# Which operand stands in the array: the experts' second product of a two-layer encoder kernel

## The chip, the cores and the metric

One Trainium2 chip, one core of it. The metric is the device time of one execution in microseconds; the profile comes from one execution that the hardware profiler recorded. Engines are named as in the profile: PE (TensorE, its weight loads apart as PEld), DVE (VectorE), ACT (ScalarE), POOL (GpSimd), SP (SyncE, which issues most of the DMAs).

## What is computed

Two encoder layers on 256 tokens of 1024 channels. Each layer is a token-mixing sub-layer and then a product-key expert sub-layer, both wrapped in a residual and a LayerNorm. The change lies in the second product of the expert sub-layer. The reference picks 16 of 16384 experts per head and token and then computes

```python
act = jax.nn.gelu(jnp.einsum('cd,chkd->chk', hc, u_tab[ic]))
w = (gc * act.astype(jnp.float32)).astype(hc.dtype)
return jnp.einsum('chk,chkd->cd', w, v_tab[ic])
...
x <- LayerNorm(ALPHA * x + gate * sublayer(x * (1 + scale) + shift))
```

The kernel does not gather: it computes all 16384 activations against the table U, multiplies them by a dense matrix of weights that is zero for experts that were not picked, and multiplies the result W (16384 experts x 256 tokens) by the table V (16384 x 1024).

## The kernel before

The program is a list of jobs (loop at L1203 to L1234). A job of a large product has a block of 128 x 1024 float32 weights in DRAM (512 KB), which SP loads into a tile `raw` (three buffers, L1171). ACT rounds it to a high part `whi` (`split_hi`, L238) and DVE computes the low part `wlo` as the difference (`split_lo`, L241); both have three buffers (LOOK + 1) and are made two jobs ahead, so ACT writes the `whi` of job k + 2 into the buffer that job k - 1 has left. Each product is taken in three passes, low x high, high x low and high x high, in float32r, all added up in PSUM. Everything between the large products (top-k, expert weights, attention) is issued in steps beside them; a scheduler of the framework puts the instructions of each engine in order, by priorities of its own, and the orders shown below are its result.

The expert sub-layer of each layer l has 16 query jobs, 128 jobs of U (`u_job`, L1038) and then 128 jobs of V (`v_job`, L1069). The 256 columns of W for each job stand in the big tiles GA, GB0, GB1 and GB2 as [expert, token]. `pre` splits one such [128, 256] block into a pair `wv` (ACT and DVE, tiles with the tags e0, e1 and pts). Then `three(m, ...)` takes channel chunk m = 0..7: the 128 x 128 block of V is the stationary operand, the 256 tokens move, and the sum stands in PSUM as [channel, token], two chunks to a bank, in banks 0 to 3 (`acc4`):

```python
o = state["acc4"][m // 2][:, m % 2]
PE.matmul(o, hi[:, m], wl, ...)
PE.matmul(o, lo[:, m], wh, ...)
PE.matmul(o, hi[:, m], wh, ...)
```

That is 24 matmuls per job, each with a weight load of its own, in L1080 to L1082. The last three jobs (VLAST) are held back and taken chunk by chunk, nine matmuls for each chunk, so that the end of the sub-layer can begin on chunk 0 while chunk 7 is multiplied. `ln2` (L1125) adds each chunk, scaled, to the residual r (L1130), and `stats` sums r and r squared over the chunks (ACT L305 and L309, DVE L311 and L315, tile `lnss`); `norm` then forms the sums over partitions on PE (L339), a Newton chain on DVE (L320 to L324), broadcasts (L327) and two passes over r (L358). In layer 1 the next layer's first products follow, in layer 2 the output.

Hooks on the V jobs carry other work: at jobs 1 and 3 `make_cact` loads the conditioning vector (`crow`, by a DMA on ACT's queue) and multiplies it out on PE (`cb`, L166), and 8 to 24 times a layer DVE forms a column of the modulation from 512 KB of `w_ada` (L260). At job 110 `load_r` claims the tile `raws`, in the space of GA, and `r`.

Of the kernel before, what the change touches and what calls it, by code (L numbers as in the profile page):

```python
# [11 lines left out]
F32 = mybir.dt.float32  # L12
# [10 lines left out]
NC8 = 8  # L23
# [3 lines left out]
NAREA = 3           # products whose weights are split ahead of a norm  # L27
NCAND = 4 * 16 + 12 * 4     # pairs (i, j) of ranks with i < 4 or j < 4: any other has more than 16 ahead of it
LATE = 320 + DEPTH * 384
VLAST = 3           # of the experts' last products, taken chunk by chunk  # L30
GSCALE = 4096.0      # on the experts' weights while they are float16 pairs

# columns of the packed parameters
# [3 lines left out]
# columns of the packed constants  # L37
# [3 lines left out]
# chunks of 128 columns of w_in  # L41
# [3 lines left out]
# order in which the chunks of the modulation are made: (scale, shift) of the first sub-layer, then the rest  # L45
# [3 lines left out]
class Background:  # L49
    """Chains of small operations, taken step by step between the large products."""  # L50
# [4 lines left out]
    def add(self, make):  # L55
        """make(lane) gives the generator of the steps"""
        self.pending.append(make)
# [12 lines left out]
    def round(self):  # L70
        """a step of each lane; false when there was none"""
        return any([self.step(i) is not None for i in range(len(self.active))])

    def run(self, budget):
        """steps for about this much time; what they took more"""
        while budget > 0:
            c = self.step(0)
            if c is None:
                return 0.0
            budget -= c  # L80
        return -budget


class InOrder:
    """an engine whose instructions keep their place among those emitted before"""
# [30 lines left out]
def _body(tc, nc, A, pp, big, hp, st, wk, ps, dr, stop, dump):  # L116
# [6 lines left out]
    # ---------------------------------------------------------------- set-up  # L123
    prm = pp.tile([128, NPRM], F32, name="prm")
    nc.sync.dma_start(prm, A["prm"])
    xd = dr.tile([128, NC8, T], F32, name="xd")      # ALPHA x, away from the chip while a sub-layer runs
# [16 lines left out]
    fold = pp.tile([128, 2, 2, NC8], F32, name="fold")   # scale and shift of the next layer's input; of the residual  # L143
# [4 lines left out]
    def make_cact(parts=(0, 1)):  # L148
        """silu(c) on all partitions"""
# [21 lines left out]
    def late_setup():  # L171
# [13 lines left out]
        # lambda of the differential attention  # L185
# [12 lines left out]
        # softplus(-lam) = max(-lam, 0) + log1p(exp(-|lam|)), log1p by the series of atanh  # L198
# [7 lines left out]
        V.tensor_tensor(w[:, 2], w[:, 1], w[:, 3], op=OP.mult)          # z  # L206
        V.tensor_tensor(w[:, 3], w[:, 2], w[:, 2], op=OP.mult)          # z^2
# [9 lines left out]
    # ---------------------------------------------------------------- helpers  # L217
# [12 lines left out]
    def drain_small():  # L230
        """what the products before the last one left"""
# [11 lines left out]
    def prod(out, whi, wlo, xhi, xlo, n, start=True, stop=True):  # L243
        """out[m, t] += sum over n chunks of w[k, c, m] x[k, c, t], in three passes"""
# [19 lines left out]
    def mains(ks):  # L264
        """banks of the large products, in turn"""
        state["banks"] = cycle(ks)
# [7 lines left out]
    def new_areas(tag, more=0):  # L274
        """room for the weights of the first products after a norm"""
# [12 lines left out]
    def behind(*ins):  # L288
        """what follows waits its turn behind these"""
# [10 lines left out]
    def stats(r, m, direct):  # L300
        """sums of r and r^2 over the chunks so far; the last chunks of r are left to norm's products"""
# [15 lines left out]
    def rsqrt(y, hv):  # L317
        """y = (2 hv)^-1/2 of two columns: Newton's steps from the exponent's estimate; each turns the sign"""
# [10 lines left out]
    def norm(r, emit):  # L329
        """(r - mean) / std in place, emit(m) after each chunk"""  # L330
# [31 lines left out]
    def norm_to_h(r, hi, lo, sc, sh, g, b):  # L362
        """h = (norm * g + b) * (1 + sc) + sh, split; xd = ALPHA (norm * g + b)"""
# [20 lines left out]
    # ---------------------------------------------------------------- jobs  # L384
# [3 lines left out]
    def areas_of(js, before, n):  # L388
        """the areas of js filled after the job n of those before, and split after each next one"""
# [36 lines left out]
    def layer(l):  # L426
        pv = lambda o, w=1: prm[:, o:o + w]

        # ------------------------------------------------ token mixing
# [65 lines left out]
        def bchunk(a, k):  # L495
            """chunk k of the branches' outputs, its high or low part"""
# [7 lines left out]
        def to_keys(e, lane):  # L504
            """p^T [key, chunk of keys, query]"""
# [24 lines left out]
        def pair(lane, branch, c):  # L530
            """two heads of the branches A and B"""
# [210 lines left out]
        # ------------------------------------------------ gated merge  # L742
# [35 lines left out]
        # the rest of the modulation, but for the gate of the experts  # L778
# [44 lines left out]
        # ------------------------------------------------ product-key experts  # L823
        def peer_begin():
# [23 lines left out]
            # over the scores, once they are ranked  # L848
# [14 lines left out]
        def top16(sets):  # L863
            """the 16 largest and their places, for independent sets in turn"""
# [27 lines left out]
        def select_gen():  # L892
# [17 lines left out]
            # the place p in cand: i = p / 16, j = p mod 16 below 64; then i = p / 4 - 12, j = p mod 4  # L910
# [19 lines left out]
            for t in range(2):  # L930
                tt = slice(t * 128, (t + 1) * 128)
                for i in range(2):
# [6 lines left out]
                    # one term of each sum is not zero  # L939
# [19 lines left out]
        def slots(lo, hi):  # L959
            """pieces of the expert columns lo..hi"""  # L960
# [7 lines left out]
        def weights_gen():  # L968
# [5 lines left out]
            def onehots(t0):  # L974
                """rows of the weights in two parts (exact to float32's last place), and columns"""
# [88 lines left out]
        def v_begin():  # L1064
            drain()
            state["acc4"] = [bank(k, [128, 2, T], name="vacc") for k in range(4)]
        jobs.append(Job(func=v_begin))

        def v_job(j):  # L1069
# [8 lines left out]
            def three(m, hi, lo, wh, wl, first, last):  # L1078
                o = state["acc4"][m // 2][:, m % 2]
# [245 lines left out]
```

## Time and profile before

| | |
|---|---|
| three runs | 2422.90, 2424.97 and 2426.39 us, median 2424.97 us |
| profiled execution | 2424.2 us from the first to the last instruction (the profile gives no other time of it) |
| PE matmul busy | 98% of the span, 19540 matmuls |
| PE weight loads busy | 95%, 19540 loads |
| DVE, ACT busy | 77% and 53% |
| V jobs, matmuls | 3 x 2048; those of L1080 start from 837.5 to 1212.4 us and from 2032.9 to 2404.4 us |

The matmul's duration in the profile (0.28 us) runs from its start to the end of its last column's way through the array, and several are under way at once; what a matmul costs in a stream is the distance from one start to the next. "PEclk" and the third column from the right of a table by stretches give the clock that was granted to TensorE: 1.00 is 2.4 GHz, 0.50 is 1.2 GHz. "<-" in brackets names who ended an engine's idle time.

### The profile page before, as it was taken

Reading aid. Unit: us, or ns where it says so; the run is one execution under the profiler, and the core shown is the slowest. Engines: PE = TensorE matmul, PEld = TensorE weight load, DVE = VectorE, ACT = ScalarE, POOL = GpSimd, SP = SyncE. Lnnn points to the kernel's source line nnn. Section 1 sums busy time; section 2 is a strip of 40 time slices with the busy share of each in tenths; the row PEclk is TensorE's granted clock in tenths of the full one; section 3 lists DMA queues with packets and bytes.
Section 4 is the critical chain, followed back from the end, with each engine's and each line's share of the span. In section 5 each row is a group of like instructions: output and inputs, shape, how many; then the busy total and the mean of one; then the engine's idle time right before and its main releaser. Section 6 shows DMA issues by size and latency. Waiting matters only on the chain.

```text
span 2424.2 us, 49848 instructions
## 1 busy us (share of the span) xinstructions
PE 2367.3 (98%) x19540; PEld 2298.4 (95%) x19540; DVE 1871.2 (77%) x4056; ACT 1281.7 (53%) x2535; POOL 0.2 (0%) x4
## 2 busy tenths in 40 slices
PE   6999999999999999999989999999999999999997
PEld 5988999999999999999988889899999999999997
DVE  8687788989999656666677877889899996655555
ACT  5755545456554444445467564455555554444443
POOL 0000000000000000000000000000000000000000
PEclk9999999999999999999989999999999999999998
DMA  8465763454444566767533756545554455655553
GB/s 328 151 210 202 252 227 130 165 190 158 157 160 157 191 205 218 243 219 261 192 132 129 263 183 244 200 149 183 167 165 158 160 165 194 219 201 184 184 200 106
DMA packets 127638, 460.64 MB, mean 190 GB/s; under 512 B 15398, under 2 KB 20006, under 8 KB 124204
## 3 DMA queue, kind: packets, MB, share of 16 engines
q1 hardware_dynamic: 126816, 453.25, 55.0%
q8 instruction: 155, 2.54, 0.4%
q10 hardware_dynamic: 588, 4.21, 0.4%
q14 instruction: 79, 0.65, 0.1%
HBM read 448.75 MB, written 5.24 MB: 187 GB/s over the span
## 4 chain that ended last, share of the span: by engine, by line
PE 85%; DVE 12%; issue 1%; ACT 1%; DMA 1%; SPq 0%; ACTq 0%; DVEq 0%
PE main L246 16%; PE main L247 16%; PE main L248 16%; PE vacc L1080 10%; PE vacc L1081 10%; PE vacc L1082 10%; DVE wlo L241 3%; PE s L520 2%; DVE topk L92 1%; DVE GA L1005 1%; PE gw L995 1%; PE o L576 1%; DVE ada L260 1%; PE gw L996 1%; DVE GB L1005 1%
## 5 line engine op out<-in xcount | busy, mean ns | idle before, releaser
L241 DVE TENSOR_TENSOR wlo<-raw,whi 128x1024 fp32r<-128x1024 f32 x723 | 879.1, 1217 | 394.0 <-ACT whi L238 390.5
L246 PE MATMUL main<-hhi,wlo 128*128 128x256 f32 x3456 | 999.5, 289 | 0.6 <-DVE wlo L241 0.6
L238 ACT ACTIVATE whi<-raw 128x1024 fp32r<-128x1024 f32 x720 | 760.7, 1057 | 436.4 <-PE vacc L1082 370.6
L247 PE MATMUL main<-hlo,whi 128*128 128x256 f32 x3456 | 978.1, 283 | 0.0
L248 PE MATMUL main<-hhi,whi 128*128 128x256 f32 x3456 | 978.1, 283 | 0.0
L246 PEld LDWEIGHTS main<-hhi,wlo 128*128 128x128 f32 x3456 | 662.4, 192 | 5.4 <-DVE wlo L241 2.2
L247 PEld LDWEIGHTS main<-hlo,whi 128*128 128x128 f32 x3456 | 662.5, 192 | 1.3 <-issue 0.8
L248 PEld LDWEIGHTS main<-hhi,whi 128*128 128x128 f32 x3456 | 661.9, 192 | 0.7 <-issue 0.7
L1080 PE MATMUL vacc<-wv,whi 128*128 128x256 f32 x2048 | 580.7, 284 | 0.0
L1081 PE MATMUL vacc<-wv,wlo 128*128 128x256 f32 x2048 | 580.6, 284 | 0.0
L1082 PE MATMUL vacc<-wv,whi 128*128 128x256 f32 x2048 | 580.5, 284 | 0.0
L1080 PEld LDWEIGHTS vacc<-wv,whi 128*128 128x128 f32 x2048 | 394.1, 193 | 2.6 <-DVE wlo L241 1.5
L1081 PEld LDWEIGHTS vacc<-wv,wlo 128*128 128x128 f32 x2048 | 394.2, 192 | 0.0
L1082 PEld LDWEIGHTS vacc<-wv,whi 128*128 128x128 f32 x2048 | 394.2, 192 | 0.0
L1052 ACT ACTIVATE gel<-main 128x256 f32<-128x256 f32 (+20 forms) x192 | 56.6, 295 | 228.2 <-PE main L248 227.7
L1009 ACT ACTIVATE GB<-gw 128x128 f32<-128x128 f32 (+15 forms) x316 | 71.9, 339 | 49.8 <-DVE GB L1005 49.4
L1005 DVE TENSOR_TENSOR GA<-gw,GA 128x256 f32<-128x256 f32 (+17 forms) x128 | 88.4, 691 | 1.2
L995 PE MATMUL gw<-ohb,oha 128*128 128x128 f16 x512 | 72.0, 222 | 1.0 <-ACT GB L1009 0.4
L247 PE MATMUL main<-mixB,whi 128*128 128x256 f32 x256 | 72.5, 283 | 0.0
L248 PE MATMUL main<-mixB,whi 128*128 128x256 f32 x256 | 72.5, 283 | 0.0
L246 PE MATMUL main<-mixB,wlo 128*128 128x256 f32 x256 | 72.5, 283 | 0.0
L724 ACT ACTIVATE mixG<-main,hbg 128x256 f32<-128x256 f32 x64 | 30.2, 472 | 76.7 <-PE main L248 76.5
(228 smaller groups left out, 2409.6 us busy)
## 6 DMA issues: line engine op xcount, KB each, us to landing
raw<-in_p_u SPq DMA_DIRECT2D x256, 512.0 KB, 3.4
raw<-in_p_v SPq DMA_DIRECT2D x256, 512.0 KB, 3.6
raw<-in_w_in SPq DMA_DIRECT2D x134, 512.0 KB, 3.9
mixA<-in_w_ada SPq DMA_DIRECT2D x48, 512.0 KB, 4.6
raw<-in_w_br SPq DMA_DIRECT2D x32, 512.0 KB, 3.8
adav<-in_w_ada SPq DMA_DIRECT2D x32, 512.0 KB, 4.4
raw<-in_p_wq SPq DMA_DIRECT2D x26, 512.0 KB, 3.5
ada<-in_w_ada SPq DMA_DIRECT2D x8, 1024.0 KB, 11.9
```

Source lines behind the costliest of these rows:

```text
L238: return S.activation(hi, src, AF.Copy, scale=scale)
L241: return V.tensor_tensor(lo, src, hi.bitcast(F32), op=OP.subtract)
L246: PE.matmul(out, wlo(c), xhi(c), start=start and c == 0, stop=False)
L247: PE.matmul(out, whi(c), xlo(c), start=False, stop=False)
L248: PE.matmul(out, whi(c), xhi(c), start=False, stop=stop and c == n - 1)
L995: PE.matmul(p[:, k], a[:, 0, k], b[:, k], start=True, stop=False)
L1005: V.tensor_tensor(o, p[:, :, x:x + n], o, op=OP.mult)
L1009: S.activation(sl[:, :, t0:t0 + NB].rearrange("p j t -> p t j"), p[:, :, x:x + n], AF.Copy)
L1052: S.activation(t[:, :n], out[:, :n], AF.Gelu_apprx_tanh)
L1080: PE.matmul(o, hi[:, m], wl, start=first and m % 2 == 0, stop=False, skip_group_check=True)
L1081: PE.matmul(o, lo[:, m], wh, start=False, stop=False, skip_group_check=True)
L1082: PE.matmul(o, hi[:, m], wh, start=False, stop=last, skip_group_check=True)
```

## The change

In the V jobs the two operands change places. The stationary operand is now a 128 x 128 block of `wv` (experts x tokens, one of two halves of the tokens), and rows of V move, 512 of their 1024 columns at a time. The sum stands in PSUM as [token, channel], one bank for each pair of token half (b % 2) and channel half (b // 2). A job takes four groups of three matmuls with 512 columns in place of eight groups of three with 256.

Because LayerNorm and all that follows want [channel, token], the four sums are copied to SBUF (`take`, ACT for b = 0 and 2, DVE for b = 1 and 3, 128 x 512 each, into 2048 more columns of `raws`) and turned by 16 transposes of 128 x 128 on PE (`turn`), into banks 4, 5, 6 and 0. `ln2` reads those. The three held jobs are taken bank by bank, and the transposes of bank b - 1 follow the matmuls of bank b.

```diff
-            state["acc4"] = [bank(k, [128, 2, T], name="vacc") for k in range(4)]
+            state["acc4"] = [bank(k, [128, 512], name="vacc") for k in range(4)]
...
-            def three(m, hi, lo, wh, wl, first, last):
-                o = state["acc4"][m // 2][:, m % 2]
-                PE.matmul(o, hi[:, m], wl, start=first and m % 2 == 0, stop=False, skip_group_check=True)
-                PE.matmul(o, lo[:, m], wh, start=False, stop=False, skip_group_check=True)
-                PE.matmul(o, hi[:, m], wh, start=False, stop=last, skip_group_check=True)
+            def three(b, hi, lo, wh, wl, first, last):
+
+                o = state["acc4"][b]
+                tt = slice(b % 2 * 128, b % 2 * 128 + 128)
+                hi, lo = (x.rearrange("p c m -> p (c m)")[:, b // 2 * 512:b // 2 * 512 + 512] for x in (hi, lo))
+                PE.matmul(o, wl[:, tt], hi, start=first, stop=False)
+                PE.matmul(o, wh[:, tt], lo, start=False, stop=False)
+                PE.matmul(o, wh[:, tt], hi, start=False, stop=last)
...
                 elif j == 127:
-                    for m in range(NC8):
+                    for b in range(4):
                         for i, x in enumerate(held):
-                            three(m, *x, False, i == VLAST - 1)
+                            three(b, *x, False, i == VLAST - 1)
+                        take(b)
+                        if b:
+                            turn(b - 1)
+                    turn(3)
...
+        def take(b):
+            out = state["raws"][:, NAREA * D + 512 * b:NAREA * D + 512 * (b + 1)]
+            if b % 2:
+                V.tensor_copy(out, state["acc4"][b])
+            else:
+                S.activation(out, state["acc4"][b], AF.Copy)
+
+        def turn(b):
+
+            if b % 2 == 0:
+                ks = (4, 5) if b == 0 else (6, 0)
+                state["turned", b // 2] = [bank(k, [128, 2, T], name="vt") for k in ks]
+            for q in range(4):
+                o = NAREA * D + 512 * b + 128 * q
+                PE.transpose(state["turned", b // 2][q // 2][:, q % 2, b % 2 * 128:b % 2 * 128 + 128],
+                             state["raws"][:, o:o + 128], ident)
+
         def load_r():
             r = new_chunks("r2")
-            new_areas("gA")
+            new_areas("gA", 2048)
...
-                V.scalar_tensor_tensor(r[:, m], state["acc4"][m // 2][:, m % 2], gq[:, m:m + 1], r[:, m],
+                V.scalar_tensor_tensor(r[:, m], state["turned", m // 4][m % 4 // 2][:, m % 2], gq[:, m:m + 1], r[:, m],
```

Where the instructions move, PE's order first: the start of a V job in the middle of layer 1, before (vacc0 and vacc1 are banks 0 and 1 of the sums).

```order
L1080 MATMUL vacc0_10939<-wv_12271,whi_12241 128x256 [waits DVE_49,Activation_49]
L1081 MATMUL vacc0_10939<-wv_12271,wlo_12242 128x256 [waits DVE_49]
L1082 MATMUL vacc0_10939<-wv_12271,whi_12241 128x256
L1080 MATMUL vacc0_10939<-wv_12271,whi_12241 128x256
L1081 MATMUL vacc0_10939<-wv_12271,wlo_12242 128x256
L1082 MATMUL vacc0_10939<-wv_12271,whi_12241 128x256
```

And the same place with the change.

```order
L1083 MATMUL vacc0_10939<-whi_11785,wv_11803 128x512 [waits DVE_49,Activation_49]
L1084 MATMUL vacc0_10939<-wlo_11786,wv_11803 128x512 [waits DVE_49]
L1085 MATMUL vacc0_10939<-whi_11785,wv_11803 128x512
L1083 MATMUL vacc1_10940<-whi_11785,wv_11803 128x512
L1084 MATMUL vacc1_10940<-wlo_11786,wv_11803 128x512
L1085 MATMUL vacc1_10940<-whi_11785,wv_11803 128x512
```

Three matmuls of 512 columns now fill a bank where six of 256 did, and the waits for ACT and DVE stand at the same two instructions of a job. The second place is PE at the end of layer 2 with the change, from the last matmuls on bank 3 (vt4, vt5, vt6 and vt0 are the turned sums in banks 4, 5, 6 and 0; cst holds the identity).

```order
L1085 MATMUL vacc3_24565<-whi_27217,wv_27233 128x512
L1083 MATMUL vacc3_24565<-whi_27236,wv_27240 128x512
L1084 MATMUL vacc3_24565<-wlo_27237,wv_27240 128x512
L1085 MATMUL vacc3_24565<-whi_27236,wv_27240 128x512
L1118 MATMUL vt6_27293<-cst_82,raws_26938 128x128 [waits Activation_49]
L1118 MATMUL vt6_27293<-cst_82,raws_26938 128x128
L1118 MATMUL vt0_27294<-cst_82,raws_26938 128x128 x2
L1118 MATMUL vt6_27293<-cst_82,raws_26938 128x128 [waits DVE_49]
L1118 MATMUL vt6_27293<-cst_82,raws_26938 128x128
L1118 MATMUL vt0_27294<-cst_82,raws_26938 128x128 x2
L339 MATMUL lnst7_27341<-ones_87,lnss_27306 128x1 [waits DVE_49]
L339 MATMUL lnst7_27341<-ones_87,lnss_27306 128x1
```

Before, the last matmul on vacc3 is followed at once by L339; now eight transposes stand between, four that wait for ACT's copy of bank 2 and four that wait for DVE's copy of bank 3. The eight of banks 0 and 1 stand ahead of bank 3's nine matmuls, behind those of bank 1 and of bank 2. The third place is DVE at the end of layer 2, before, from the last split to where its work on r and the sums over chunks repeats.

```order
L241 TENSOR_TENSOR wlo_30249<-raw_30157,whi_30248 128x1024 [waits DMAHW7_49,Activation_49]
L1130 SCALAR_TENSOR_TENSOR r2_29780<-vacc0_26074,gq_30327,r2_29780 128x256 [waits PE_49]
L1130 SCALAR_TENSOR_TENSOR r2_29780<-vacc0_26074,gq_30327,r2_29780 128x256
L1130 SCALAR_TENSOR_TENSOR r2_29780<-vacc1_26075,gq_30327,r2_29780 128x256 [waits PE_49]
L1130 SCALAR_TENSOR_TENSOR r2_29780<-vacc1_26075,gq_30327,r2_29780 128x256
L1130 SCALAR_TENSOR_TENSOR r2_29780<-vacc2_26076,gq_30327,r2_29780 128x256 [waits PE_49]
L1130 SCALAR_TENSOR_TENSOR r2_29780<-vacc2_26076,gq_30327,r2_29780 128x256
L311 TENSOR_TENSOR lnss_30330<-r2_29780 128x256 [waits DVE_49,PE_49]
L1130 SCALAR_TENSOR_TENSOR r2_29780<-vacc3_26077,gq_30327,r2_29780 128x256 [waits PE_49]
L315 TENSOR_TENSOR lnss_30330<-lnss_30330,sq_30333 128x256 [waits Activation_49]
L311 TENSOR_TENSOR lnss_30330<-lnss_30330,r2_29780 128x256 [waits DVE_49]
L315 TENSOR_TENSOR lnss_30330<-lnss_30330,sq_30338 128x256 [waits DVE_49]
```

And with the change.

```order
L241 TENSOR_TENSOR wlo_27237<-raw_27181,whi_27236 128x1024 [waits DMAHW7_49,Activation_49]
L1107 COPY raws_26938<-vacc1_24563 128x512 [waits PE_49]
L1154 SCALAR_TENSOR_TENSOR r2_26936<-vt4_27263,gq_27303,r2_26936 128x256 [waits PE_49]
L1154 SCALAR_TENSOR_TENSOR r2_26936<-vt4_27263,gq_27303,r2_26936 128x256
L1154 SCALAR_TENSOR_TENSOR r2_26936<-vt5_27264,gq_27303,r2_26936 128x256 [waits PE_49]
L1154 SCALAR_TENSOR_TENSOR r2_26936<-vt5_27264,gq_27303,r2_26936 128x256
L311 TENSOR_TENSOR lnss_27306<-r2_26936 128x256 [waits DVE_49,PE_49]
L315 TENSOR_TENSOR lnss_27306<-lnss_27306,sq_27309 128x256 [waits Activation_49]
L1107 COPY raws_26938<-vacc3_24565 128x512 [waits PE_49]
L311 TENSOR_TENSOR lnss_27306<-lnss_27306,r2_26936 128x256 [waits DVE_49]
L315 TENSOR_TENSOR lnss_27306<-lnss_27306,sq_27314 128x256 [waits DVE_49]
L311 TENSOR_TENSOR lnss_27306<-lnss_27306,r2_26936 128x256 [waits DVE_49]
```

DVE's first work on r now waits for the transposes that follow bank 2, the copy of bank 3 stands behind four chunks of r and two sums, and the other four chunks of r come behind that copy, where one chunk was left before.

## Rows read from the trace of the kernel before

**Rows 1.** The page: the span, and the granted clock in 40 slices.

```profile
span 2424.2 us, 49848 instructions
...
PEclk9999999999999999999989999999999999999998
```

**Rows 2.** The page: the chain that ended last, its shares by line.

```profile
PE main L246 16%; PE main L247 16%; PE main L248 16%; PE vacc L1080 10%; PE vacc L1081 10%; PE vacc L1082 10%; DVE wlo L241 3%; PE s L520 2%; DVE topk L92 1%; DVE GA L1005 1%; PE gw L995 1%; PE o L576 1%; DVE ada L260 1%; PE gw L996 1%; DVE GB L1005 1%
```

**Rows 3.** The page, costliest groups: one line of the V matmuls.

```profile
L1081 PE MATMUL vacc<-wv,wlo 128*128 128x256 f32 x2048 | 580.6, 284 | 0.0
```

**Rows 4.** Table by stretches: busy us of each engine (instructions), PEclk, DMA share, GB/s.

```profile
1000.00:1100.00 100.00, 100.00 (x836) 100.00 (x835) 65.87 (x87) 50.08 (x73) 0.00 (x0) 1.00 0.69 237
1220.00:1228.00 8.00, 4.29 (x19) 3.90 (x20) 7.46 (x27) 4.25 (x10) 0.00 (x0) 0.50 0.20 67
```

**Rows 5.** Timeline of PE, V jobs: start us, duration us, instruction.

```profile
1000.10 0.28 PE L1080 MATMUL vacc<-wv,whi 128*128 128x256 f32 x1
1000.22 0.28 PE L1081 MATMUL vacc<-wv,wlo 128*128 128x256 f32 x1
```

**Rows 6.** Timeline of PE at half clock: first and last of five.

```profile
1225.85 0.41 PE L248 MATMUL main<-hhi,areas 128*128 128x256 f32 x1
...
1226.70 0.41 PE L248 MATMUL main<-hhi,areas 128*128 128x256 f32 x1
```

**Rows 7.** Timeline of PE, U jobs, around float16 matmuls.

```profile
561.20 0.22 PE L996 MATMUL gw<-ohb,oha 128*128 128x128 f16 x1
...
561.54 0.22 PE L996 MATMUL gw<-ohb,oha 128*128 128x128 f16 x1
...
561.77 0.28 PE L247 MATMUL main<-hlo,whi 128*128 128x256 f32 x1
...
562.12 0.28 PE L247 MATMUL main<-hlo,whi 128*128 128x256 f32 x1
```

**Rows 8.** Timeline of weight loads: four with one-column matmuls, then the next.

```profile
225.44 0.54 PEld L623 LDWEIGHTS stc<-ones,sqc 128*128 128x128 f32 x4
225.90 0.19 PEld L246 LDWEIGHTS main<-hhi,wlo 128*128 128x128 f32 x1
```

**Rows 9.** Chain of waits, ordinary float32: start us, us, what.

```profile
70.34 0.86 PE z L654 x4
...
93.62 0.87 PE pt L509 x8
```

**Rows 10.** Timeline of ACT and DVE in one V job.

```profile
999.58 1.06 ACT L238 ACTIVATE whi<-raw 128x1024 fp32r<-128x1024 f32 x1 [1.52 <-PE vacc L1082]
...
1000.54 0.40 ACT L238 ACTIVATE wv<-GA 128x256 fp32r<-128x256 f32 x1
...
1000.67 1.22 DVE L241 TENSOR_TENSOR wlo<-raw,whi 128x1024 fp32r<-128x1024 f32 x1 [1.32 <-ACT whi L238]
...
1001.81 0.42 DVE L241 TENSOR_TENSOR wv<-GA,wv 128x256 fp32r<-128x256 f32 x1
```

**Rows 11.** The page, DMA issues: blocks of V, KB each, us to landing.

```profile
raw<-in_p_v SPq DMA_DIRECT2D x256, 512.0 KB, 3.6
```

**Rows 12.** Timeline of DVE at the end of layer 2.

```profile
2404.94 0.48 DVE L1130 SCALAR_TENSOR_TENSOR r<-vacc,gq,r 128x256 f32<-128x256 f32 x1
2405.34 0.42 DVE L315 TENSOR_TENSOR lnss<-lnss,sq 128x256 f32<-128x256 f32 x1
...
2409.38 0.42 DVE L315 TENSOR_TENSOR lnss<-lnss,sq 128x256 f32<-128x256 f32 x1 [0.21 <-ACT sq L309]
```

**Rows 13.** Timeline of PE, last V matmul of layer 2.

```profile
2404.62 0.28 PE L1082 MATMUL vacc<-wv,whi 128*128 128x256 f32 x1
```

**Rows 14.** Groups by form: evictions from PSUM on ACT and DVE.

```profile
L510 ACT ACTIVATE e<-pt 128x512 f32<-128x512 f32 x40 | 22.8, 593 | 13.7 <-PE pt L509 13.6
...
L482 DVE COPY mixA<-vt 128x256 f32<-128x256 f32 x18 | 7.5, 419 | 13.9 <-PE vt L481 13.9
```

**Rows 15.** Chain of waits, conditioning vector in layer 2.

```profile
2038.90 2.95 DMA crow<-in_c
```

More of the change, by code (lines that the diff above doesn't have):

```diff
@@ L1086, in mm @@
                 if j < 128 - VLAST:
-                    for m in range(NC8):
-                        three(m, *held[-1], j == 0, False)
+                    for b in range(4):
+                        three(b, *held[-1], j == 0, False)
                     held.clear()
                 elif j == 127:
-                    for m in range(NC8):
+                    for b in range(4):
                         for i, x in enumerate(held):
-                            three(m, *x, False, i == VLAST - 1)
+                            three(b, *x, False, i == VLAST - 1)
[3 more added lines that the diff above has]
+                    turn(3)
             return Job(src=A["p_v"][l, j], mm=mm, pre=pre)
         held = []
+        def take(b):
[12 more added lines that the diff above has]
+                             state["raws"][:, o:o + 128], ident)
         def load_r():
             r = new_chunks("r2")
-            new_areas("gA")
+            new_areas("gA", 2048)
             nc.sync.dma_start(r, xd)
```

## The prediction, made before the changed kernel ran

> **What bounds the kernel now.** I read the page first. The span is 2424.2 us and the clock is full in nearly every slice [rows 1]; the median of the three runs, 2424.97 us, lies 0.8 us above it, and the sum below is made against the span. Of the chain that ended last, the three lines of V matmuls hold 10% each [rows 2], about 730 us: they bound their stretch. Each line has 2048 matmuls, 6144 in all [rows 3]. In 100 us of a V stretch 836 matmuls start and PE is never idle [rows 4]; start follows start in 0.12 us, a matmul of 256 columns and a load of 128 columns each time [rows 5]. So the question is what fills these 0.120 us.
>
> **What a matmul's 0.120 us are.** At half clock (0.50 in [rows 4]) five matmuls of the same shape start 0.85 us apart, 0.2125 us each [rows 6]: 256 columns at one column a cycle of 1.2 GHz (0.2133), nothing left over. At 2.4 GHz the columns take 0.1067, so 0.0133 us of the 0.120 are something else. In float16, with 128 columns, six steps take 0.34 us, 0.0567 each [rows 7], where the columns take 0.0533: 0.003 left over. The 0.0133 is therefore peculiar to float32r at full clock. Three readings are left. (a) It comes once per matmul and its load, when the array changes from one set of weights to the next. (b) The load is the bound and hides under a longer stream. (c) It comes with the columns, since a stream of 4-byte columns at full clock cannot quite be fed.
>
> For (b): four loads with one-column matmuls beside them take 0.46 us, 0.115 each [rows 8], near 0.120, but less. And in ordinary float32, where a column takes two cycles, 256 columns (0.2133) with a load each start 0.86 / 4 = 0.215 apart [rows 9]: under a stream as long as the new one a load costs 0.002. Against (c): just after the float16 matmuls three steps of float32r take 0.35 us, 0.117 each [rows 7], with the same number of columns, so not all of the 0.0133 is tied to them. Against (b) taken whole: the loads alone are shorter than 0.120.
>
> **The sum.** The change takes 6144 matmuls of 256 columns away and adds 3072 of 512. The columns moved are as many as before; the number of loads is halved. By (a) a new matmul costs 0.2133 + 0.0133 = 0.2267 us, by (b) 0.215, by (c) 0.240. I take (a): it is between the ends, and the rows beside it speak against either end taken whole. Gain: 3072 x (0.240 - 0.2267) = **-40.9 us**. The ends are 3072 x 0.025 = -76.8 and 0.
>
> The Trainium skill (TensorE: Matmul & The Clock Gate, section Back-to-back issue gap) gives an isolated distance of N / 2.4 + 2.5 ns, which is 109 ns for 256 columns and 216 ns for 512. By that rule two short matmuls would cost 218 and one long one 216, and the change would gain only 3072 x 2.5 ns = 7.5 us, hardly more than the turning back costs; but the trace has 0.120 us and not 0.109 at 256 columns, so the rule's own start is refuted here, and no row shows its 512.
>
> What feeds PE must keep up. A V job would take 12 x 0.2267 = 2.72 us in place of 2.88. Per job ACT has 1.06 + 0.40 us, and DVE 1.22 + 0.42 [rows 10], with a column of the modulation in every fifth job; ACT's idle time before its split is ended by PE, so both follow PE, not the other way. The next block but two is asked for when the low part is done, 2.3 us into a job, and is needed 3 x 2.72 = 8.2 us later than the job's start: 5.9 us for a landing of 3.6 [rows 11]. At 0.69 of the DMA engines' time [rows 4] a pace that is 6% higher needs 0.73. Cost nothing; were a block late, its wait would show on ACT first.
>
> Turning back, PE's side: eight of a layer's 16 transposes stand before the last nine matmuls. Float32 transposes of this shape take 0.87 / 8 = 0.109 us [rows 9]: 0.87 us. The other eight run while DVE is the one waited for.
>
> The Trainium skill (same page, Part 4: PE-mode transpose) names about 275 ns for a 128 x 128 transpose in a kernel's context. At that price the eight on the path of each layer would cost 2.7 us more over both; the row has 0.109 us from start to start.
>
> Turning back, DVE's side. Before, 2409.80 - 2404.62 = 5.2 us pass from the last matmul's start to the end of the last sum of squares [rows 12, 13], and DVE is busy in nearly all of it. With the change its queue holds, when the last matmul starts, the last two chunks of r and two sums (0.75 us), then a copy of 512 columns. A copy of 256 out of PSUM takes 0.42 [rows 14] and DVE's 1024 columns take 1.22 where 256 take 0.42 [rows 10], so 512 cost some 0.69; the nearest whole row is ACT's eviction at 0.59 [rows 14]. Behind it PE turns bank 3 (0.44 + some 0.2 until seen), in which DVE does four sums (4 x 0.335 = 1.35), then four chunks of r (0.40 each when they follow one another) and six sums, with a wait for ACT's last square (0.4): 1.6 + 2.0 + 0.4. That is 0.75 + 0.69 + 1.35 + 4.0 = 6.8 us, **+1.6 us**. Layer 1 has ACT's split of the next block (1.06) ahead of the squares, but DVE has its queue to work off meanwhile. With the transposes each layer's end grows by 2.5 us, 5.0 in all. The ends: 1.7 us, if DVE absorbs everything, and 8, if copy, turning and r run one behind the other.
>
> One small loss: at job 3 PE waits for the conditioning vector, whose DMA (2.95 us in layer 2 [rows 15]) starts when job 1 leaves its buffer; the job in between covers 0.16 us less, twice: +0.3.
>
> Sum: -40.9 + 5.0 + 0.3 = -35.6, span 2388.6, time **2389 us**.
>
> **The rivals.** *The loads were the bound* (b): 0.215 a matmul, or up to 0.220 if a load leaves some of its trace even under the long stream, -77 to -61, with the ends 2353 to 2369 us. For it speaks [rows 9], and that loads alone come near 0.120; against it, that they are shorter. The Trainium skill's 216 ns for 512 columns (section named above) is this case's time too, and only a run can tell. *Between (a) and (c)*: half of the 0.0133 goes with the columns, 0.2333 a matmul, -20.6, 2410 us. *The columns were the bound* (c), the one that ends slower: PE cannot take 4-byte columns any faster than 256 in 0.120 us, the long matmul costs 0.240, nothing is gained and the turning back is all that is left: 2424.97 + 5.3 = 2430 us. With these ends it is slower from 0.2383 on, and by more than 0.2% (4.8 us, about what a measurement of this kernel can tell from no change) from 0.2398, or from 0.2389 if the ends cost 8 us in place of 5. For it speaks that at half clock nothing is left over; against it, the 0.117. That the change does nothing of what it says is excluded: PE's order has 3072 matmuls fewer, 32 transposes more.
>
> **How the numbers follow.** Chances: (a) 0.45; (b) 0.28; between (a) and (c) 0.15; (c) 0.12. The time is that of (a). The range goes from 2355, nearly all of (b), to 2416, which takes in the case between with the dearer ends; it leaves out (c) and a little on either side, some 0.18. Faster by over 0.2%: all but (c) and the edge of the case beside it, 0.87. (c) lies on the bound: 0.06 the same, 0.07 slower.
>
> **What would show it.** In the changed profile: starts of V matmuls 0.227 us apart, some 440 in 100 us, PE never idle in the V stretch; 0.215 is (b), 0.240 is (c). At each layer's end, DVE's copy of bank 3 about 0.75 us after the last V matmul's start, transposes 0.109 apart, and the first L339 some 7 us after it. The prediction would be wrong in its reasoning, whatever the time, if PE had idle gaps in the V stretch (blocks, splits or `wv` late), or if the end of a layer grew by more than 4 us.

## The result, and the profile after

The changed kernel takes **2384.68 us** (median of four runs, 2382.79 to 2385.74). The kernel before, on the same chip, takes 2425.31 us (four runs). The ratio is 0.9837 with a 95% interval of 0.9825 to 0.9849: faster by 1.6%, some 40 us. Forecast were 2389 us and a gain of 36.

The V stretch after, in the view by stretches that [rows 4] shows of before (columns: busy time of PE, PE's weight loads, DVE, ACT and POOL with the number of instructions, granted clock, share of the DMA engines, GB/s):

```profile
900.00:1000.00 100.00, 100.00 (x443) 82.81 (x442) 66.48 (x92) 50.36 (x74) 0.00 (x0) 1.00 0.67 230
1000.00:1100.00 100.00, 100.00 (x442) 82.80 (x442) 69.12 (x91) 52.72 (x77) 0.00 (x0) 1.00 0.72 256
```

443 and 442 matmuls fall into 100 us where 836 did, PE never idle, and PE's loads no longer busy all the time (82.8 where it was 100). The spacing itself, in PE's timeline after (columns: start, duration, both in us, engine, line, operation, tiles, shapes), where [rows 5] stood before:

```profile
1000.06 0.39 PE L1083 MATMUL vacc<-whi,wv 128*128 128x512 f32 x1
1000.29 0.39 PE L1084 MATMUL vacc<-wlo,wv 128*128 128x512 f32 x1
1000.51 0.39 PE L1085 MATMUL vacc<-whi,wv 128*128 128x512 f32 x1
1000.74 0.39 PE L1083 MATMUL vacc<-whi,wv 128*128 128x512 f32 x1
```

Three steps take 0.68 us. Over the 882 starts from 900 to 1100 us the mean is 0.22667 us: 512 columns at 2.4 GHz (0.21333) and 0.01333 more. The record of a load now has room before it (groups of weight loads after; columns: count, busy us, mean ns, idle us before them):

```profile
L1084 PEld LDWEIGHTS vacc<-wlo,wv 128*128 128x128 f32 x1024 | 192.7, 188 | 40.0 <-DVE wlo L241 0.5
```

The first and the last V matmul of layer 1, the first V matmul of layer 2, then layer 2's seam, on PE's timeline:

```profile
836.31 0.40 PE L1083 MATMUL vacc<-whi,wv 128*128 128x512 f32 x1
...
1190.03 0.39 PE L1085 MATMUL vacc<-whi,wv 128*128 128x512 f32 x1
...
2011.72 0.40 PE L1083 MATMUL vacc<-whi,wv 128*128 128x512 f32 x1
...
2358.64 0.39 PE L1085 MATMUL vacc<-whi,wv 128*128 128x512 f32 x1
2358.88 0.60 PE L1118 MATMUL vt<-cst,raws 128*128 128x128 f32 x4
2359.23 0.48 PE L1083 MATMUL vacc<-whi,wv 128*128 128x512 f32 x1
...
2363.70 0.39 PE L1085 MATMUL vacc<-whi,wv 128*128 128x512 f32 x1
2363.93 0.60 PE L1118 MATMUL vt<-cst,raws 128*128 128x128 f32 x4
2365.02 0.66 PE L1118 MATMUL vt<-cst,raws 128*128 128x128 f32 x4 [0.50 <-DVE raws L1107]
```

And DVE behind the last V matmul of layer 2, which answers to [rows 12]:

```profile
2364.28 0.68 DVE L1107 COPY raws<-vacc 128x512 f32<-128x512 f32 x1
2364.89 0.42 DVE L311 TENSOR_TENSOR lnss<-lnss,r 128x256 f32<-128x256 f32 x1
...
2368.35 0.87 DVE L1154 SCALAR_TENSOR_TENSOR r<-vt,gq,r 128x256 f32<-128x256 f32 x2
2369.37 0.95 DVE L315 TENSOR_TENSOR lnss<-lnss,sq 128x256 f32<-128x256 f32 x2
```

The spans are 2424.2 and 2384.0 us, 40.2 apart. Cut at these matmuls (before: 837.49, 1212.64, 2032.94 and 2404.62), the difference lies in five pieces: ahead of layer 1's V matmuls -1.2 (836.31 against 837.49), layer 1's V matmuls -21.4 (353.7 against 375.2), from there to layer 2's +1.4 (821.7 against 820.3), layer 2's V matmuls -19.7 (352.0 against 371.7), the rest +0.7 (20.3 against 19.6). All of the gain but the 1.2 us ahead is in the two V stretches, and both seams behind them give a little back. The piece ahead of layer 1 is the granted clock: 49 us into the kernel the change is already 1.4 us ahead, with the same instructions. Until then the profile of before has the clock at 0.50 twice, from 29.0 to 32.5 and from 39.3 to 42.7 us, and the profile of the change has it at 1.00 there.

### The profile page after: what moved, and what is told of

Read it like the earlier page. It is cut to its first block, busy times and chain, and to the rows that moved or that the text cites. A ratio compares the mean times of both kernels' runs of the same rounds, so it can differ in the third digit from the quotient of the medians.

```text
span 2384.0 us, 43786 instructions
## 1 busy us (share of the span) xinstructions
PE 2329.0 (98%) x16500; PEld 2138.7 (90%) x16500; DVE 1872.0 (79%) x4060; ACT 1285.3 (54%) x2539; POOL 0.2 (0%) x4
## 4 chain that ended last, share of the span: by engine, by line
PE 85%; DVE 12%; issue 1%; ACT 1%; DMA 1%; SPq 0%; ACTq 0%; DVEq 0%
PE main L246 16%; PE main L247 16%; PE main L248 16%; PE vacc L1083 10%; PE vacc L1084 10%; PE vacc L1085 10%; DVE wlo L241 4%; PE s L520 2%; DVE topk L92 1%; DVE GA L1005 1%; PE gw L995 1%; PE o L576 1%; DVE ada L260 1%; PE gw L996 1%; DVE GB L1005 1%
## 5 line engine op out<-in xcount | busy, mean ns | idle before, releaser
L1083 PE MATMUL vacc<-whi,wv 128*128 128x512 f32 x1024 | 399.6, 391 | 0.0
L1084 PE MATMUL vacc<-wlo,wv 128*128 128x512 f32 x1024 | 399.2, 390 | 0.0
L1085 PE MATMUL vacc<-whi,wv 128*128 128x512 f32 x1024 | 398.9, 390 | 0.0
L1083 PEld LDWEIGHTS vacc<-whi,wv 128*128 128x128 f32 x1024 | 192.4, 188 | 41.7 <-DVE wv L241 1.5
L1085 PEld LDWEIGHTS vacc<-whi,wv 128*128 128x128 f32 x1024 | 192.6, 188 | 40.3
L1084 PEld LDWEIGHTS vacc<-wlo,wv 128*128 128x128 f32 x1024 | 192.7, 188 | 40.0 <-DVE wlo L241 0.5
L1057 ACT ACTIVATE GA<-main 128x256 f32<-128x256 f32 x64 | 24.6, 385 | 87.6 <-PE main L248 87.5
```

What stands on the lines that cost most here:

```text
L1083: PE.matmul(o, wl[:, tt], hi, start=first, stop=False)
L1084: PE.matmul(o, wh[:, tt], lo, start=False, stop=False)
L1085: PE.matmul(o, wh[:, tt], hi, start=False, stop=last)
```

## The experiments

The theory at the start was (a): 13.3 ns for each float32r matmul at full clock, whatever its width; halving the number of matmuls takes half of them away. Seven kernels were run beside the kernel before and the change. The fourth of them edits the kernel before; the others edit the changed kernel, the last one also in the other products.

| kernel | us | ratio to before, 95% interval |
|---|---|---|
| the change | 2384.68 | 0.9837 (0.9825 to 0.9849) |
| rows of V in pieces of 256 | 2432.21 | 1.0033 (1.002 to 1.0047) |
| in pieces of 384 and 128 | 2574.89, one run | |
| float16 pairs in the V jobs, on the change | 2353.60 | 0.9715 (0.9699 to 0.9732) |
| float16 pairs in the V jobs, on before | 2357.94 | 0.9736 (0.9718 to 0.9754) |
| no turning back | 2383.86 | 0.9821 (0.9808 to 0.9834) |
| 64 columns of weights | 2399.40, one run | |
| float16 pairs in all large products | 2266.58 | 0.9341 (0.9327 to 0.9356) |

**Pieces of 256 columns.** The operands stay exchanged and the turning back stays; only the width goes back. This parts the width from the exchange.

```diff
-                PE.matmul(o, wl[:, tt], hi, start=first, stop=False)
+                for x, y in ((0, 256), (256, 512)):
+                    PE.matmul(o[:, x:y], wl[:, tt], hi[:, x:y], ...)
...
```

> The changed kernel, but V's rows move 256 columns at a time (two pieces per bank), with the tokens' weights still in the array and the turning back kept. Theory (a), 0.0133 us once per float32r matmul whatever its width: V matmuls 0.120 us apart as before the change, 3072 x 0.0133 = 41 us are given back, about 2425 us. Rival, the gain comes from which operand stands and which moves, not from the width: the distance per 512 columns stays near 0.227 us and the time near 2385 us.

Its PE timeline at 1000 us:

```profile
1000.00 0.28 PE L1086 MATMUL vacc<-whi,wv 128*128 128x256 f32 x1
1000.12 0.28 PE L1084 MATMUL vacc<-whi,wv 128*128 128x256 f32 x1
1000.24 0.28 PE L1085 MATMUL vacc<-wlo,wv 128*128 128x256 f32 x1
```

The starts are 0.120 us apart again (mean of 1667 starts: 119.999 ns), with V's rows moving and `wv` standing. For this distance it does not matter which operand stands; the width makes all of the difference. The time, 0.2 to 0.5% above before, is that of the kernel before with the turning back on top. It is some 7 us more than the 2425 or so that (a) gives, and not the rival's 2385. The profiled run (2429.95 us, span 2428.1) shows 2.2 of them: some 24 V matmuls of layer 2 fell into a stretch at half clock (0.213 us apart), behind the stall for the conditioning vector, which the kernel before did not have there. The row of that stretch follows; the rest of the difference stays open.

```profile
2044.40:2049.60 5.20, 5.20 (x25) 5.20 (x26) 2.17 (x5) 0.90 (x2) 0.00 (x0) 0.50 0.33 101
```

**Pieces of 384 and 128 columns.** The same edit with `((0, 384), (384, 512))`: as many matmuls as with 256, as many columns, but unequal.

> The changed kernel, each bank taken in a piece of 384 and one of 128 columns, each with its own load. Theory (a) with the load hidden: 0.1733 and 0.0667 us, together 0.240 in place of 0.227, about 2426 us. Rival, the load of 128 columns is itself a floor (alone it took 0.115 us a piece in the kernel before): 0.173 and 0.115 to 0.120 us, together 0.29, 3072 x 0.064 = 195 us more, about 2580 us. A third reading, that short float32r matmuls take two or four cycles a column: 0.107 to 0.213 us for the piece of 128 columns, 2540 to 2860 us.

PE's timeline, one round of six matmuls, and the loads that belong to it:

```profile
1000.18 0.40 PE L1084 MATMUL vacc<-whi,wv 128*128 128x384 f32 x1
1000.42 0.34 PE L1085 MATMUL vacc<-wlo,wv 128*128 128x384 f32 x1
1000.60 0.34 PE L1086 MATMUL vacc<-whi,wv 128*128 128x384 f32 x1
1000.77 0.22 PE L1084 MATMUL vacc<-whi,wv 128*128 128x128 f32 x1
1000.83 0.27 PE L1085 MATMUL vacc<-wlo,wv 128*128 128x128 f32 x1
1000.94 0.28 PE L1086 MATMUL vacc<-whi,wv 128*128 128x128 f32 x1
1001.05 0.39 PE L1084 MATMUL vacc<-whi,wv 128*128 128x384 f32 x1
```

```profile
1000.77 0.19 PEld L1085 LDWEIGHTS vacc<-wlo,wv 128*128 128x128 f32 x1
1000.88 0.19 PEld L1086 LDWEIGHTS vacc<-whi,wv 128*128 128x128 f32 x1
1000.99 0.19 PEld L1084 LDWEIGHTS vacc<-whi,wv 128*128 128x128 f32 x1
1001.10 0.19 PEld L1085 LDWEIGHTS vacc<-wlo,wv 128*128 128x128 f32 x1
```

A round takes 0.868 us here and 0.863 in the mean of 231 rounds. The columns alone would take 0.64, and with 13.3 ns for each matmul 0.72. The loads say why it is more: beside the short pieces they come 0.11 us apart, one after the other, and a matmul of 128 columns (0.053 us) is over long before the next load is. So the loads are a floor of their own, 0.11 to 0.115 us each, as [rows 8] had it. The six steps of a round are 0.230, 0.175, 0.175, 0.060, 0.111 and 0.112 us in the mean: the steps behind the second and the third short piece are as long as a load, and the 0.230 behind the first piece of 384 is 0.055 longer than the two that follow it. The 2574.89 us are near the 2580 of the rival on record and not the 2426 of (a). They lie within the third reading too (two cycles a column for short matmuls, from 2540 us on); against it stands the step of 0.060 us behind the first short piece, where two cycles a column would take 0.107. At 256 columns the stream (0.107 + 0.013) is just above this floor; at 128 it is far below, at 512 it is out of sight. That is the part of truth in rival (b): the floor exists, but it is not what 256 columns ran against.

**Float16 pairs in the V jobs**, on the change and on the kernel before: the same split into a high and a low part, rounded to float16 in place of float32r. In float32r slow loads and the 13.3 ns come together; in float16 both are smaller (the record of a load is 98 ns long there and 188 in the change).

```diff
-                w = wk.tile([128, 2, T], F32R, name="wv", ...)
+                w = wk.tile([128, 2, T], F16, name="wv", ...)
...
-                hi = st.tile([128, NC8, 128], F32R, name="whi", ...)
+                hi = st.tile([128, NC8, 128], getattr(j, "dt", F32R), name="whi", ...)
...
```

> The changed kernel with float16 pairs in place of float32r pairs in the V jobs (high part and difference, both operands), all else the same. Theory: the 0.0133 us belong to float32r at full clock, float16 leaves 0.002 to 0.003 over (0.0567 us for 128 columns in the kernel before), so 0.216 us a matmul, 3072 x 0.011 = 34 us less, about 2351 us. Rival, any change of weights costs a full-clock matmul 0.0133 us: no change, about 2385 us. A second one: the splits or DMAs cannot follow at 2.6 us a job and PE gets gaps: between the two.

> The kernel before the change with float16 pairs in the V jobs, V in the array and 256 tokens moving. Theory: 0.109 us a matmul in place of 0.120, 6144 x 0.011 = 67 us less, about 2358 us; the exchange of the operands would then be worth only about 3 us (e3 against this), since float16 has almost nothing to save per matmul. Rival, the cost goes with the matmul and not with the type: no change, 2425 us.

Groups of V matmuls, of the float16 kernel with the change and of the one without (columns: count, busy us, mean ns, idle us before):

```profile
L1084 PE MATMUL vacc<-wlo,wv 128*128 128x512 f16 x1024 | 388.8, 380 | 0.0
```

```profile
L1081 PE MATMUL vacc<-wv,wlo 128*128 128x256 f16 x2048 | 558.2, 273 | 0.7 <-DVE wlo L241 0.7
```

The starts are 215.8 ns apart with 512 columns (927 starts) and mostly 109 with 256 (mean 109.8 over 1822 starts, in which two short waits for `wlo` lie): 2.5 ns beyond the columns in both. So in float16 the exchange takes 3072 x 2.5 = 7.7 us off, the ends give part of that back, and the medians differ by 4.3 us, with intervals that overlap. In float32r the same edit is worth 40 us. What the change saves is the 13.3 ns, and those belong to float32r. Whether they belong to the moving rows or to the weights these two runs do not part, since both change type together. What float16 pairs do to the accuracy of the result is not measured here.

**No turning back.** `take`, `turn` and the 16 transposes of a layer are left out, and the sums of squares and layer 2's residual read the accumulators as they stand.

```diff
-                        take(b)
-                        if b:
-                            turn(b - 1)
-                    turn(3)
...
-                V.scalar_tensor_tensor(r[:, m], state["turned", m // 4][m % 4 // 2][:, m % 2], gq[:, m:m + 1], ...
+                V.scalar_tensor_tensor(r[:, m], state["acc4"][m // 2][:, m % 2 * T:m % 2 * T + T], gq[:, m:m + 1], ...
```

> Leaves out the turning back: the four copies of the sums and the 32 transposes are gone, and the sums of squares and layer 2's residual read the accumulators as they stand (the wrong way round). What is left of the change is its V matmuls alone. The prediction's terms give 2384.7 - 5.0 = 2379.7 us for it. The trace of the change, added up at the two seams, gives ends of about 3.9 us in both layers together, so about 2380.8 us. Rival: the turning back is hidden at layer 1's seam (the next product's loads and the normalization wait for something else there), and only layer 2's end pays: then 2382 to 2383 us. If the ends cost over 8 us (below 2376.5 us), the matmuls gave less than 40.9 us and the prediction was right only by two errors.

2383.86 us, 3 more than expected and nearer to the rival's 2382 to 2383, but the kernel before took 2426.81 us beside it, 1.5 more than beside the change. The ratios to before, 0.9821 here and 0.9837 with the turning back, differ by 0.0016 or 3.9 us; their intervals overlap, so the times alone do not show it. The trace does. DVE at the end of layer 2 without the turning back, whose last V matmul starts at 2360.57:

```profile
2360.32 0.42 DVE L311 TENSOR_TENSOR lnss<-r 128x256 f32<-128x256 f32 x1 [0.48 <-PE vacc L1085]
...
2363.85 0.87 DVE L1150 SCALAR_TENSOR_TENSOR r<-vacc,gq,r 128x256 f32<-128x256 f32 x2
2364.88 0.95 DVE L315 TENSOR_TENSOR lnss<-lnss,sq 128x256 f32<-128x256 f32 x2 [0.15 <-ACT sq L309]
```

From the last V matmul's start to the end of the last sum of squares 5.26 us pass (2365.83 - 2360.57). With the turning back it is 6.62 (2370.32 - 2363.70), before the change 5.18: 1.4 us of DVE and PE for the last bank. In layer 1 it is 1.3 (6.45 against 5.16). The eight transposes ahead of the last matmuls of a layer cost 0.9 in PE's stream: the last nine matmuls of bank 2 and of bank 3 take 2.52 and 2.53 us in layer 2 with them, and 2.06 and 2.04 without; in layer 1 it is 2.50 and 2.52 against 2.06 and 2.04. (Layer 2's V matmuls as a whole, 352.0 and 351.2 us, are only 0.8 apart, because the stall for the conditioning vector is 0.2 longer without the turning back.) From the last V matmul's start to the first use of the finished sums by DVE (L342) the two kernels are 1.1 us apart in layer 1 and 1.2 in layer 2, so the rival, that layer 1's seam hides the turning back, falls. A layer pays 0.9 + 1.15, and both some 4.2 us; the ratios say 3.9. The granted clock has a part in the 1.15: without the turning back it goes to 0.50 at 3.2 and 3.3 us after the last V matmul of a layer, ahead of nearly all of the sums over partitions (L339), and with it only at 5.5 and 6.0.

**64 columns of weights.** From the second V job of a layer on, only the first 64 tokens of a block are loaded; half of the sums are left out, and every matmul still moves 512 columns.

```diff
+                if not first:
+                    tt, o = slice(tt.start, tt.start + 64), o[:64]
                 PE.matmul(o, wl[:, tt], hi, start=first, stop=False, skip_group_check=True)
```

> After the first V job of a layer only the first 64 tokens of each block are loaded as weights (64 columns instead of 128), so half the tokens' sums are left out from there on; the 512 moving columns of every matmul stay. What is asked: whether the 13.3 ns that a float32r matmul takes beyond its columns belong to its weight load's size. If they are the same for every float32r matmul at full clock, the starts stay 226.7 ns apart and the time stays at about 2384 us. If they go with the columns loaded, the starts come 220.0 ns apart (half of 13.3), which takes 3048 x 6.7 ns = 20 us off: about 2364 us. If they come from something of the moving operand, 226.7 as well, so this run only tells for or against the load.

```profile
999.92 0.13 PEld L1087 LDWEIGHTS vacc<-whi,wv 128*64 128x64 f32 x1
1000.15 0.13 PEld L1085 LDWEIGHTS vacc<-whi,wv 128*64 128x64 f32 x1
```

The load's record shrinks from 188 to some 130 ns, so the load is shorter by half of its 115 ns. The matmuls do not come closer: their starts are 230.0 ns apart in the mean (870 starts; single ones between 224 and 236), 3.3 ns further than with full loads, and the kernel takes 2399.4 us. Neither distance on record came out, 226.7 or 220.0: what is left beyond the columns is 16.7 ns, more and not less. So the 13.3 ns do not shrink with the size of the load. What makes a half load 3.3 ns worse stays open.

**Float16 pairs in all large products**, to see how far the finding carries: `whi`, `wlo`, `hhi`, `hlo`, `mixB` and `areas` become float16 as well, on top of the change.

> All float32r pairs of the program (the V jobs' and those of every other large product) are float16 pairs instead; the order of the work is as in the change. Going by the two float16 kernels, a matmul takes 2.5 ns beyond its columns instead of 13.3, so each of the 11,424 matmuls of 256 columns gives 10.8 ns (120.0 to 109.2) and each of the 3,072 of 512 columns gives 10.8 (226.7 to 215.8): 123.7 + 33.3 = 157 us, so 2384.7 - 157 = 2228 us. Rival: a job of 512 KB then lasts 2.6 us everywhere, and the transfers, which already keep the DMA engines busy for 0.76 of the V stage in float16, don't keep up in the stages that load something besides: then TensorE waits and the time is 2240 to 2290 us.

2266.58 us, the fastest of all, 6.6% below before, but 39 us above what the sum gave. The V stretches keep their 216 ns. Most of the loss is in the two stretches that hold the U jobs, and it is neither the DMA engines (0.54 and 0.53 of their time) nor PE. First these stretches with the U jobs in the kernel with the change, then the like stretches in float16:

```profile
400.00:836.00 436.00, 435.36 (x3869) 431.57 (x3868) 397.56 (x1005) 232.97 (x565) 0.00 (x0) 1.00 0.49 168
1560.00:2012.00 452.00, 451.33 (x4003) 447.50 (x4002) 409.08 (x1058) 243.83 (x586) 0.00 (x0) 1.00 0.49 167
```

```profile
400.00:790.00 390.00, 375.78 (x3650) 334.07 (x3648) 368.37 (x904) 218.19 (x542) 0.00 (x0) 1.00 0.54 176
1470.00:1905.00 435.00, 420.16 (x4037) 373.16 (x4035) 408.20 (x1071) 246.61 (x599) 0.00 (x0) 1.00 0.53 174
```

PE's idle time rises from 1.3 to 29.1 us in these two, and DVE goes from 91% to 94% busy. What PE waits for from 400 to 790 us (view of waits; columns: us in all, times, longest), and what stands behind the first of them on ACT:

```profile
PE gw L995 <- ACT GB L1009: 5.9, 7, 1.3
PE main L246 <- DVE wlo L241: 4.3, 8, 0.7
PE gw L995 <- DVE oha L981: 3.3, 4, 1.0
```

```profile
ACT GB L1009 <- DVE GB L1005: 57.3, 36, 3.1
```

These three are 13.5 of the 14.2 us, and each goes back to DVE, directly or over ACT. ACT also waits for blocks of U, 5.2 us in all from 400 to 790, but DVE had no pause of 0.15 us or more in the 7 us before any wait of PE of 0.3 us and more, in either stretch. With shorter matmuls DVE's part of a U job has become nearly as long as PE's: busy for 368.4 us of 390 where PE is for 375.8. The rival on record had the right sign and the wrong engine.

## Why the prediction was right

**Which reading of the 0.120 us.** Step (a) was right to the nanosecond: 0.2267 us was forecast for a matmul of 512 columns and 0.22667 is the mean of the trace. Of the rivals, (b) falls on the number of starts (0.215 would have been 465 in 100 us; there are 443 and 442), and so do the case between (0.2333: 429) and (c) (0.240: 417). The runs with pieces say more: 13.3 ns at 256 columns and at 512, and 15 at 384 (0.175 us from one to the next in the middle of a round), so they do not grow with the columns; and with half the load they do not shrink. "Once per matmul" is what all three widths have in common. It is a mean of a steady stream and not a fixed charge on each matmul: behind the first piece of 128 columns the step is 0.060 us, 6.7 ns beyond its columns, and with half loads single steps lie between 224 and 236 ns. What in the array takes them is open: no run here has a float32r matmul without a load of its own.

The Trainium skill (TensorE: Matmul & The Clock Gate, section Back-to-back issue gap) gives N / 2.4 + 2.5 ns as the isolated distance at full clock. The float16 kernels agree with it, 109 ns and 215.8 ns, and the float32r ones do not, 120.0 and 226.7: for float32r the measured 13.3 ns take the place of its 2.5. Had the kernel been in float16, its forecast for this change (7.5 us of gain, less what the turning back costs) would have been near: the two float16 kernels are 4.3 us apart.

**The gain in matmuls.** Forecast -40.9 us over both layers. Layer 2's V matmuls gave -19.7; without the 0.9 of its transposes that is -20.7, where half of 40.9 is 20.5. Layer 1 gave -21.4, 1.7 more than layer 2, and that is not the change's doing: behind the stall for the conditioning vector PE ran at half clock from 848.2 to 855.1 us before and from 847.4 to 850.8 after. Before, 22 V matmuls took 0.213 us in place of 0.120 there (2.05 us), and the stall itself 4.33 us, 1.41 more than in layer 2; after, it is some 1.7 and 0.2. The difference is 1.6 us. Where such a stretch comes, and how long it is, differs from kernel to kernel (none in either layer without the turning back, one of 6.8 us in layer 2 with pieces of 256), so a change of this kernel by 2 us cannot be read off one profile.

**The ends.** Forecast +5.0; against the kernel before +4.0 (0.9 twice, 1.4 and 0.7). DVE's "+1.6 us" a layer is the term that came out smaller, and nearly all of that in layer 2. Up to the last sum of squares it was nearly good: the copy of 512 columns takes 0.68 us (0.69 forecast), comes 0.58 us after the last matmul's start (0.75 forecast), and the last sum of squares of layer 2 is done after 6.6 us (6.8), 1.4 later than before, in layer 1 1.2 later. What the term left out is the step behind it: DVE then waits for PE to add up the sums over partitions (L339). In layer 1 that wait hardly changes (0.50 us before, 0.75 with the change), and 1.4 us arrive at L342. In layer 2 it was 1.97 us before the change and is 1.10 with it, so only 0.6 us arrive. The row before the change, and the one after:

```profile
2411.77 0.16 DVE L342 TENSOR_SCALAR lnw<-lnst 128x2 f32<-128x2 f32 x1 [1.97 <-PE lnst L339]
```

```profile
2371.43 0.16 DVE L342 TENSOR_SCALAR lnw<-lnst 128x2 f32<-128x2 f32 x1 [1.10 <-PE lnst L339]
```

In layer 2 the difference is the granted clock. Eight of PE's matmuls of L339 and a stretch in which they start, before, and then with the change (columns of the stretch as above, the clock third from the right):

```profile
2409.03 1.85 PE L339 MATMUL lnst<-ones,r 128*128 128x1 f32 x8
2409.00:2412.00 3.00, 2.73 (x13) 2.65 (x13) 0.82 (x4) 0.34 (x1) 0.00 (x0) 0.50 0.00 0
```

```profile
2368.88 1.13 PE L339 MATMUL lnst<-ones,r 128*128 128x1 f32 x8
2368.80:2369.70 0.90, 0.82 (x8) 0.82 (x8) 0.75 (x3) 0.78 (x2) 0.00 (x0) 1.00 0.00 0
```

Before, PE had done nothing since the last V matmul, the clock went to 0.50 at 2408.1 us, and these matmuls start 0.21 us apart; with the change eight transposes stand in between, the clock stays at 1.00 until 2369.7, and they start 0.11 apart. The float16 kernel without the change ends its last sum of squares of layer 2 after 5.18 us, as the kernel before does, but its clock falls 1.8 us later: it reaches L342 6.20 us after its last V matmul, the kernel before 7.15, the change 7.73. So some 0.9 of the 1.0 us by which the ends came out cheaper is the granted clock in one profile, and not the work that the prediction priced. One sign that it named did not come: the first matmul of L339 starts 4.8 and 4.5 us after the last V matmul and not some 7, because it adds up r and does not need the squares; the four for the squares start at 6.8 and 6.7.

PE's transposes were right: 0.87 us forecast for the eight on a layer's path, 0.9 measured. They start 0.109 us apart, as forecast, and not 0.27, the length of one record.

**The stall for the conditioning vector.** Forecast +0.3. Layer 2 shows nothing of it: 2921 ns from one V matmul to the next across it, 2915 before. In layer 1 it went from 4329 to 3119 ns: the last 2.1 us of the old one ran at half clock, nothing of the new one. The term was within what these stretches do by themselves.

**The other engines.** PE is never idle in the V stretch, the DMA engines' share is 0.72 (0.73 forecast) and no block came late: right, and in float16, with a job of 2.6 us, still right but for two waits for `wlo` of 0.7 us in all without the change. Where the cover is thin is the U stretch, which the change does not touch and the last experiment does.

Summed with what was measured: -41.3 (twice the matmuls of layer 2) + 4.0 - 1.6 (half clock) - 1.2 (ahead of the first V matmul, where nothing was changed) = -40.1 of -40.2 us. Of the 4.6 us by which the gain was larger than forecast, 0.4 are the matmuls, 1.0 the cheaper ends, 0.3 the stall, and 2.8 the last two terms, which are not the change's. With the 0.9 in the ends, 3.7 of the 4.6 us are the times at which the clock was at half in these two profiles. The medians of four runs lie 40.6 us apart, so the other runs gave about as much; there is no trace of them.

## What to carry to other kernels

Cut the distance between starts into columns and remainder at both clocks and in both types before costing a change of a matmul's width: what remains per matmul is what wider matmuls save, here 13.3 ns in float32r and 2.5 in float16. With the remainder so unequal, the number format can be worth more than the shape (in the V jobs 66 us without the exchange, where the exchange alone is worth 40; 118 us on top of the exchange with all products); but after each step ask which engine has the next longest share of a job, since here it was DVE and not the DMA engines. A turn of the result costs what it puts between the last matmuls (0.9 us a layer here) and what stands behind the last one (1.4 and 0.6).

## What was not expected of the hardware

- The remainder of 13.3 ns in float32r is the same at 256 and 512 columns and nearly the same (15) at 384, and gone at half clock (0.427 us for 512 columns, where 512 / 1.2 is 0.427). With 64 columns of weights in place of 128 the starts came 3.3 ns further apart, 230.0 in place of 226.7.
- Loads of 128 columns of float32r have a floor of 0.11 us each that shows as soon as the stream beside them is shorter: behind the second and the third piece of 128 columns the step is 0.111 us and not 0.067, and the matmul of 384 that follows takes 0.230 in place of 0.175.
- The granted clock behind the same stall of about 3 us fell for 6.8 us, for 3.4 us or not at all, from one kernel to the next. Behind the last V matmul of a layer it fell after 3.2 to 6.1 us in the kernels here.
